# A hybrid attention layer on one core: all projected strips go through DRAM, all local heads run beside a three-pass output projection

## The chip, the cores and the metric

The kernel runs on one core of a Trainium2 chip. The metric is the time of one execution in microseconds (us) of device time, the median of several runs. The engines of a core work side by side, each in the order of its own instruction stream: TensorE (PE in the profile, with its weight loads as PEld), VectorE (DVE), ScalarE (ACT), GpSimd (POOL) and SyncE (SP). Every DMA of this kernel is issued by SP, one after the other.

## The reference

One encoder layer is applied to two sequences, a prompt of 1024 tokens and a sample of 256, each with 16 meta tokens ahead. All is float32.

```python
u = rms_norm(h, norm_w) @ w_in                    # 2048 -> 6656 = 52 strips of 128 columns
qa, ka, va, za, qb, kb, vb, zb = split(u)         # 8, 2, 2, 8, 8, 8, 8, 8 strips
qa, ka = rope(rms_norm(qa)), rope(rms_norm(ka))
ya = global_gqa(qa, ka, va) * silu(za)            # 8 heads over 2 key heads, every key
qb, kb = rms_norm(qb), rms_norm(kb)
yb = neighbourhood_attention(qb, kb, vb, rpb) * silu(zb)   # 8 heads, 8x16 window + bias + meta
return h + concat([ya, yb]) @ w_out               # 2048 -> 2048
```

## The kernel before

**Precision.** A float32 product is made as three matmuls in a rounded format: each operand is split into a high part and a low part (`split`: a cast on ACT, L65, and a subtraction on DVE, L66), and high by high, high by low and low by high are added in PSUM. Plain float32 matmuls stand only where the local heads multiply probabilities by values (L558, L618).

**First half of the projection** (`first_half`). The 16 tiles of 128 model rows are cut in two. The product of the first eight with all 52 weight strips is formed pair of strips by pair of strips with a seven-product scheme (`strassen`, matmuls L108 to L110, PSUM pool `pa`, sums by DVE at L219), and the partial sums go to DRAM (`ud`). Ahead of it `operands` loads the input (halves x1 and x2, 16 tiles each), squares on ACT (L156), adds the squares up on DVE (L158), sums over partitions on POOL (L98) and builds seven operand matrices. Beside it the generator `ahead` works off units of its own: 32 that normalise and split the second eight input tiles into DRAM (`xd`), and 64 that load, split and store the second-half weights of 32 of the 52 strips (`ws`, `wd`). These two-buffer units share DVE, ACT and SP with the products.

**Second half and attention** (`second_half`). A strip is finished by `project`: eight tiles by three token blocks (256 or 272, 512, 512), matmuls L336 to L338, then the kept sum is added (L341) and the strip is normalised (q, k), passed through silu (z) or transposed (v). Weights of the 32 strips in `AHEAD` come split from `wd`; those of the other 20 are loaded raw into the evacuation pool `ev` (7 buffers) and split there. The 8 global heads run in order, five blocks of 256 queries each (`attend`), with q, z, k and v in SBUF; after each head up to three strips of the last six local heads are projected, and these alone go to DRAM. Then the first two local heads are projected and run, and the remaining late strips follow.

**Output projection** (`outproj`). Two passes over 16 column strips: pass 0 takes the 8 global heads, pass 1 the 8 local ones, matmuls L855 to L857. The 30 blocks of the six late local heads are spread over the first 13 strips of pass 0. At strip 13 the attention pools are closed, and the local heads' results are loaded.

**What orders the work.** A scheduler that simulates the engines puts each engine's instructions in order before anything runs; the program order is its priority. At run time each engine, and SP's queue of DMAs, keeps that order: an instruction that waits holds up all that stand behind it on its engine. The kept sums `u` have four buffers (`pu`), so the load of the next one waits until an evacuation has let one go.

Of the kernel before, what the change touches and what calls it, by code (L numbers as in the profile page):

```python
# [40 lines left out]
NL = 6  # L41
FILL_A = 3
LSTR = 13
YORD = (0, 4, 1, 5, 2, 6, 3, 7)
# [9 lines left out]
AHEAD = [KA, VA, *range(ZA, ZA + 4), *range(QA, QA + 4), KA + 1, VA + 1, *range(ZA + 4, ZA + 8), *range(QA + 4, QA + 8)]  # L54
for _h in range(NH - NL, NH - NL + 3):
    AHEAD += [KB + _h, QB_ + _h, VB + _h, ZB + _h]


class Kern:
    def __init__(self, tc, io):  # L60
        self.tc, self.nc, self.io = tc, tc.nc, io

# [30 lines left out]
    def token_scale(self, half):  # L93

        nc = self.nc
        acc = self.rb[half]
        (m, r), (l, _) = self.stage("b22", 2 * half), self.stage("b22", 2 * half + 1)
        nc.gpsimd.partition_all_reduce(m, acc[:], P, RED.add)  # L98
        self.rsqrt(m, r, l)
        nc.scalar.mul(acc[:], r, -1.0)  # L100
# [41 lines left out]
    def operands(self):  # L142
# [5 lines left out]
        raw = [[self.stage(n, k) for n in ("t2", "t3")] for k in range(WCH)]  # L148
        for half in range(2):
            for kt in range(KT):  # L150
# [4 lines left out]
                acc = self.rb[half][:]  # L155
                nc.scalar.activation(sq if kt else acc, r, AF.Square, scale=DM ** -0.5)  # L156
                if kt:
                    nc.vector.tensor_tensor(out=acc, in0=acc, in1=sq, op=ALU.add)  # L158
            self.token_scale(half)
# [22 lines left out]
        for k in range(WCH):  # L182
            t2, t4 = self.stage("b22", k)
            minus(t2, norm(1, 1, k), raw[k][0][0])
            minus(t4, raw[k][0][1], t2)
            put("t2", k, t2)
            put("t4", k, t4)
        for k in range(WCH):
            b22 = raw[k][1][1]
            put("b22", k, b22)  # L190
            t3 = self.ct("t3")[:]
            minus(t3, b22, raw[k][1][0])
            put("t3", k, t3)

# [57 lines left out]
    def ahead(self):  # L252
# [17 lines left out]
        for s in AHEAD:  # L270
            for c in range(2):
                t = self.ps.tile([P, 2, WCH, P], F32R, tag="ps", name="ws")
                nc.sync.dma_start(t[:, 1].bitcast(F32), self.io["w_in"][s][:, KH + WCH * c:KH + WCH * c + WCH, :])
                self.split_tile(t)
                nc.sync.dma_start(self.wd[s][:, c], t[:].bitcast(F32))
                yield

    def first_half(self):
# [3 lines left out]
        full = [self.mixed(0, [self.wraw(self.raw, "raw") for _ in range(4)]), self.mixed(1, [t[:, j] for t in more for j in range(2)])]  # L282
        self.operands()
# [6 lines left out]
        units = 4 * KH + 2 * len(AHEAD)  # L290
        n, done = NW // 2 - 2, 0
        for i in range(n):
# [6 lines left out]
            while done * (n - 1) < units * (i + 1) and next(ahead, self) is not self:  # L299
                done += 1  # L300
# [9 lines left out]
    def weights(self, s):  # L310
        nc = self.nc
        ws = []
        with self.tc.high_priority(offset=self.woff):
            for c in range(2):
                if s in AHEAD:
                    w = self.w.tile([P, 2, WCH, P], F32R, tag="w", name="w")
                    self.lastw = nc.sync.dma_start(w[:].bitcast(F32), self.wd[s][:, c]).ins
                else:
                    w = self.wsplit(self.wload(self.wraw(self.ev, "ev"), s, 2 + c))
                ws.append(w)  # L320
        return ws
# [22 lines left out]
    def project(self, s, blocks, evac, result=None):  # L344

        ws, us = self.weights(s), self.kept(s, blocks)
# [5 lines left out]
        return result  # L352

    def project_two(self, *parts):

        ps = [[self.pp.tile([P, 512], F32, tag="pp", name="pp") for _ in range(n)] for n in (3, 1)]
        ps[1] += [self.sp.tile([P, 512], F32, tag="sp", name="pp") for _ in range(2)]
        ws = [self.weights(p[0]) for p in parts]
        for kt in range(KH):
            for p, w, part in zip(ps, ws, parts):  # L360
                for b, (o, n) in zip(p, part[1]):
                    self.tile_products(b, w, kt, o, n)
        for p, (s, blocks, evac, _) in zip(ps, parts):
            for j, ((o, n), u, b) in enumerate(zip(blocks, self.kept(s, blocks), p)):
                evac(j, self.add_kept(b, u, n), o, n)
        return [p[3] for p in parts]
# [4 lines left out]
    def qk_evac(self, u, o, n, wc, rope, hi, lo):  # L371
# [17 lines left out]
        if lo is None:  # L389
            nc.sync.dma_start(hi, r[:])  # L390
        else:
            self.split(hi, lo, r[:])
# [8 lines left out]
    def z_evac(self, u, n, dst):  # L401
# [7 lines left out]
        nc.vector.tensor_tensor(out=dst, in0=u[:], in1=a[:], op=ALU.mult)  # L409

    def meta_scores(self, pm, meta, qh, ql, scale):
# [3 lines left out]
        nc.tensor.matmul(pm, kh, qh, start=True, stop=False)  # L415
        nc.tensor.matmul(pm, kh, ql, start=False, stop=False)
        nc.tensor.matmul(pm, kl, qh, start=False, stop=True)
# [29 lines left out]
    def put_y(self, po, tot, zs, ydst):  # L447
# [8 lines left out]
        if len(zs.shape) == 3:  # L456
            nc.vector.tensor_tensor(out=y[:].rearrange("p (g r) -> p g r", g=4), in0=po[:].rearrange("p (g r) -> p g r", g=4),
                                    in1=zs, op=ALU.mult)
        else:
            nc.vector.tensor_tensor(out=y[:], in0=po[:], in1=zs, op=ALU.mult)  # L460
# [7 lines left out]
    def attend(self, q, zs, keys, meta, vals, vmeta, ydst):  # L468
# [6 lines left out]
        for p in range(nt // 2):  # L475
            ps = self.sp.tile([P, 2, QB], F32, tag="sp", name="sp")
            for i in range(2):
                kh, kl = keys[2 * p + i]
                nc.tensor.matmul(ps[:, i, :], kh, qh, start=True, stop=False)
                nc.tensor.matmul(ps[:, i, :], kh, ql, start=False, stop=False)  # L480
                nc.tensor.matmul(ps[:, i, :], kl, qh, start=False, stop=True)
# [28 lines left out]
        tot = self.all_sum(a1, sm)  # L510
        po = self.op.tile([P, QB], F32, tag="po", name="po")
        for j in range(nt):
            p, i = divmod(j, 2)
            if i == 0:
                ph = self.ph.tile([P, 2, QB], F32R, tag="ph", name="ph")
                pl = self.ph.tile([P, 2, QB], F32R, tag="pl", name="pl")
# [3 lines left out]
            nc.tensor.matmul(po[:], vl, ph[:, i, :], start=False, stop=False)  # L520
            nc.tensor.matmul(po[:], vh, pl[:, i, :], start=False, stop=False)
        nc.tensor.matmul(po[:], vmeta, pm3[:], start=False, stop=True)
        self.put_y(po, tot, zs, ydst)

    def attend_sample(self, q, zs, k, meta, vals, vmeta, tab, ydst):
# [4 lines left out]
        for w, w0 in enumerate(WIN0):  # L530
            o, c = NMETA + 32 * w0, slice(64 * w, 64 * w + 64)
            kh, kl = k[:, 0, o:o + P], k[:, 1, o:o + P]
            nc.tensor.matmul(ps[:, 0, c], kh, qh[:, c], start=True, stop=False)
            nc.tensor.matmul(ps[:, 0, c], kh, ql[:, c], start=False, stop=False)
            nc.tensor.matmul(ps[:, 0, c], kl, qh[:, c], start=False, stop=True)
# [17 lines left out]
        tot = self.all_sum(a1, sm)  # L553
        po = self.op.tile([P, QB], F32, tag="po", name="po")
        nc.tensor.matmul(po[:], vmeta, pm3[:], start=True, stop=False)
# [464 lines left out]
```

## Time and profile before

| | |
|---|---|
| three runs | 2688.16, 2689.86 (median), 2693.88 us |
| profiled execution | 2689.95 us, of which the span is 2687.8 us |
| busy | PE 2294.1, PEld 2071.1, DVE 1755.0, ACT 1057.3, POOL 509.3 us |
| DMA | 381.81 MB, 44.1% of 16 engines' span |
| mean granted TensorE clock | 0.930 |

The profiled execution is 0.09 us over the median. The busy time of PE is a union of modelled, overlapping matmuls: back to back, a matmul of 512 columns is listed with 0.39 us though the next starts 0.23 us later. A rate is therefore read from the starts. The granted clock is 1.0 or 0.5 at each moment, and a value between them in a table is a mean over a stretch.

### The profile page before, as it was taken

To read this page: it belongs to the slowest core of one execution; us is meant where nothing else is said; L and a number is where in the kernel's file an instruction comes from. 1 tells how busy PE (TensorE), PEld (TensorE's weight loads), DVE (VectorE), ACT (ScalarE), POOL (GpSimd) and SP (SyncE) were. 2 spreads that over 40 slices of the span, in tenths; PEclk is the share of its full clock that TensorE was granted. 3 is DMA by queue.
4 is the path that set the end of the run, shared out by engine and by line. 5 is a ranking of instruction groups with operands and counts; after the bars stand their busy time and mean duration, and the time that the engine had idled before them with its cause. 6 is when DMAs were issued, how large, how long until landed. Compare 5 with 4: busy or idle time off the path is not lost.

```text
span 2687.8 us, 36415 instructions
## 1 busy us (share of the span) xinstructions
PE 2294.1 (85%) x13294; PEld 2071.1 (77%) x13294; DVE 1755.0 (65%) x3096; ACT 1057.3 (39%) x2102; POOL 509.3 (19%) x250
## 2 busy tenths in 40 slices
PE   0698989899999999899678888885868999855999
PEld 0698888899998888788566777775757888755888
DVE  6866555555536989889787887885465666673221
ACT  5322333322214656556454655554333333332000
POOL 0000000000002334333233241323131122231000
PEclk9799999999999999999888899987888999956999
DMA  5166777743256333434213233222327656534432
GB/s 199 38 201 187 266 263 272 255 135 101 95 208 216 119 104 115 124 93 144 74 46 109 76 100 91 75 70 58 94 72 293 215 175 186 188 108 184 156 130 81
DMA packets 245939, 384.14 MB, mean 143 GB/s; under 512 B 64064, under 2 KB 153088, under 8 KB 242688
## 3 DMA queue, kind: packets, MB, share of 16 engines
q1 hardware_dynamic: 245760, 381.81, 44.1%
q8 instruction: 105, 1.72, 0.3%
q14 instruction: 74, 0.61, 0.1%
HBM read 236.41 MB, written 138.74 MB: 140 GB/s over the span
## 4 chain that ended last, share of the span: by engine, by line
PE 49%; DMA 19%; DVE 17%; ACT 6%; issue 4%; POOL 2%; SPq 2%; DVEq 0%; ACTq 0%; POOLq 0%
PE pp L336 5%; PE pp L855 5%; PE pp L856 5%; PE pp L857 5%; PE pp L337 5%; PE pp L338 5%; DMA ws<-in_w_in 4%; DMA wr<-in_w_in 4%; DMA wd<-ws 3%; PE pa L108 3%; PE pa L109 3%; PE pa L110 3%; DMA xs<-in_x 1%; PE po L618 1%; DVE l L78 1%
## 5 line engine op out<-in xcount | busy, mean ns | idle before, releaser
L336 PE MATMUL pp<-x,w 128*128 128x512 f32 (+2 forms) x1248 | 463.2, 372 | 79.8 <-ACT w L65 66.9
L337 PE MATMUL pp<-x,w 128*128 128x512 f32 (+2 forms) x1248 | 459.6, 369 | 0.0
L338 PE MATMUL pp<-x,w 128*128 128x512 f32 (+2 forms) x1248 | 449.3, 365 | 0.0
L65 ACT CAST w<-wr 128x512 fp32r<-128x512 f32 x286 | 172.2, 618 | 434.2 <-PE pp L857 203.3
L336 PEld LDWEIGHTS pp<-x,w 128*128 128x128 f32 x1248 | 246.7, 198 | 119.9 <-ACT w L65 71.6
L108 PE MATMUL pa<-t,w 128*128 128x320 f32 (+1 forms) x832 | 263.0, 317 | 40.2 <-DVE u L219 14.7
L375 POOL PARTITION_ALL_REDUCE ms<-l x78 | 228.1, 2925 | 316.0 <-ACT l L374 262.3
L855 PE MATMUL pp<-yh,w 128*128 128x512 f32 (+1 forms) x768 | 275.9, 359 | 14.0 <-DMA yh<-yd 14.0
L856 PE MATMUL pp<-yh,w 128*128 128x512 f32 (+1 forms) x768 | 275.3, 359 | 0.0
L857 PE MATMUL pp<-yh,w 128*128 128x512 f32 (+1 forms) x768 | 274.5, 358 | 0.0
L337 PEld LDWEIGHTS pp<-x,w 128*128 128x128 f32 x1248 | 246.4, 198 | 32.7
L66 DVE TENSOR_TENSOR w<-wr,w 128x512 fp32r<-128x512 f32 x286 | 194.9, 688 | 114.2 <-ACT w L65 113.8
L338 PEld LDWEIGHTS pp<-x,w 128*128 128x128 f32 x1248 | 241.4, 194 | 32.8
L108 PE MATMUL pa<-b,w 128*128 128x320 f32 (+1 forms) x624 | 199.1, 320 | 77.9 <-ACT b L65 60.4
L109 PE MATMUL pa<-t,w 128*128 128x320 f32 (+1 forms) x832 | 259.5, 312 | 4.3 <-DVE t L66 4.3
L110 PE MATMUL pa<-t,w 128*128 128x320 f32 (+1 forms) x832 | 259.2, 312 | 0.0
L444 POOL PARTITION_ALL_REDUCE tot<-a x80 | 169.4, 2117 | 420.2 <-DVE a L442 420.2
L109 PE MATMUL pa<-b,w 128*128 128x320 f32 (+1 forms) x624 | 196.1, 314 | 2.3 <-DVE b L66 2.3
L110 PE MATMUL pa<-b,w 128*128 128x320 f32 (+1 forms) x624 | 195.3, 313 | 0.0
L108 PEld LDWEIGHTS pa<-t,w 128*128 128x128 f32 x832 | 158.1, 190 | 46.2 <-ACT w L65 12.7
L108 PEld LDWEIGHTS pa<-b,w 128*128 128x128 f32 x624 | 119.8, 192 | 82.2 <-ACT b L65 60.8
L427 POOL PARTITION_ALL_REDUCE ma<-m x80 | 101.2, 1266 | 429.5 <-DVE m L425 418.6
(179 smaller groups left out, 5066.0 us busy)
## 6 DMA issues: line engine op xcount, KB each, us to landing
wr<-in_w_in SPq DMA_DIRECT2D x144, 256.0 KB, 3.7
wd<-ws SPq DMA_DIRECT2D x64, 512.0 KB, 3.3
w<-wd SPq DMA_DIRECT2D x64, 512.0 KB, 4.6
u<-ud SPq DMA_DIRECT2D x104, 256.0 KB, 2.9
yd<-yt SPq DMA_DIRECT2D x160, 128.0 KB, 2.1
yh<-yd SPq DMA_DIRECT2D x16, 1280.0 KB, 16.6
ud<-c SPq DMA_DIRECT2D x52, 320.0 KB, 2.6
ws<-in_w_in SPq DMA_DIRECT2D x64, 256.0 KB, 3.6
```

What stands on the lines that cost most here:

```text
L65: nc.scalar.copy(hi, full)
L66: nc.vector.tensor_tensor(out=lo, in0=full, in1=hi.bitcast(F32), op=ALU.subtract)
L108: self.nc.tensor.matmul(p, wh, xh, start=first, stop=False)
L109: self.nc.tensor.matmul(p, wh, xl, start=False, stop=False)
L110: self.nc.tensor.matmul(p, wl, xh, start=False, stop=last)
L336: self.nc.tensor.matmul(ps[:, :n], wh, xh, start=first, stop=False)
L337: self.nc.tensor.matmul(ps[:, :n], wh, xl, start=False, stop=False)
L338: self.nc.tensor.matmul(ps[:, :n], wl, xh, start=False, stop=last)
L375: nc.gpsimd.partition_all_reduce(ms[:], l[:], P, RED.add)
L855: nc.tensor.matmul(p[:, :n], wh, yh[:, o:o + n], start=i == 0, stop=False)
L856: nc.tensor.matmul(p[:, :n], wh, yl[:, o:o + n], start=False, stop=False)
L857: nc.tensor.matmul(p[:, :n], wl, yh[:, o:o + n], start=False, stop=i == 7)
```

## The change

- **Start.** x1 is loaded ahead of the first weights. Squares are added in pairs on DVE and summed over partitions by plain float32 matmuls with a matrix of ones; the reduction on POOL is gone. One operand (t4) takes a way through DRAM (`td`).
- **No weights ahead.** The 64 `ws` units leave the first half. All 52 strips load raw weights in the second half (a pool `raw` of three buffers) and split them there. The 32 input units are spread two to a pair of strips.
- **All strips to DRAM.** q and k leave split (`qd`, `kd`), v transposed (`vt`), z as it is (`zd`). An attention block loads its own 256 queries and gates (`q_load`, four buffers); keys and values are loaded once per head or group.
- **Order of the second half.** All 40 blocks of global heads are interleaved one by one with the strips; all 32 local strips are projected here, and no local block is run.
- **Probabilities by values in plain float32.** `attend` no longer splits probabilities and values: one float32 matmul per key tile in place of three.
- **Output projection in three passes** of 6, 6 and 4 heads. The 40 local blocks run beside the first two passes, 20 each, cut in two (scores, then values) at a `yield`; their matmuls and those of the passes keep the program's order (`keep_in_program_order`). Partial sums are stored and loaded once more.

The diff, cut to its core:

```diff
+OUT = ((0, 1, 2, 3, 4, 5), (6, 7, 8, 9, 10, 11), (12, 13, 14, 15))
+YTAG = (0, 1, 2, 3, 4, 5, 6, 7, 8, 0, 1, 2, 3, 4, 5, 6)
+BLOCKS = (20, 20, 0)
+    def matmul(self, *a, **kw):
+        i = self.nc.tensor.matmul(*a, **kw)
+        if self.pin:
+            self.tc.keep_in_program_order(i)
...
-                nc.scalar.activation(sq if kt else acc, r, AF.Square, scale=DM ** -0.5)
-                if kt:
-                    nc.vector.tensor_tensor(out=acc, in0=acc, in1=sq, op=ALU.add)
-            self.token_scale(half)
+                nc.scalar.activation(sq, r, AF.Square, scale=DM ** -0.5)
+                if kt % 2:
+                    nc.vector.tensor_tensor(out=sq, in0=sq, in1=before, op=ALU.add)
+                    for b in range(2):
+                        nc.tensor.matmul(sums[:, b, :HB], ones, sq[:, b], start=kt == 1, stop=kt == KT - 1)
+                before = sq
+            self.token_scale(half, sums)
+            if half == 0:
+                full = raws()
...
-        for s in AHEAD:
-            for c in range(2):
-                t = self.ps.tile([P, 2, WCH, P], F32R, tag="ps", name="ws")
...
-            while done * (n - 1) < units * (i + 1) and next(ahead, self) is not self:
+            while done < 2 * (i + 1) and next(ahead, self) is not self:
...
     def weights(self, s):
+        with self.tc.high_priority(offset=self.woff):
+            return [self.wsplit(self.wload(self.wraw(self.raw, "raw"), s, 2 + c)) for c in range(2)]
...
+        self.split(l[:].bitcast(F32R), r[:].bitcast(F32R), r[:])
+        for i, f in enumerate((l, r)):
+            nc.sync.dma_start(dst[:, i], f[:])
...
         tot = self.all_sum(a1, sm)
+        yield
         po = self.op.tile([P, QB], F32, tag="po", name="po")
         for j in range(nt):
-            p, i = divmod(j, 2)
-            if i == 0:
...
-                self.split(ph[:], pl[:], S[p][:])
-            vh, vl = vals[j]
-            nc.tensor.matmul(po[:], vh, ph[:, i, :], start=j == 0, stop=False)
-            nc.tensor.matmul(po[:], vl, ph[:, i, :], start=False, stop=False)
-            nc.tensor.matmul(po[:], vh, pl[:, i, :], start=False, stop=False)
+            self.matmul(po[:], vals[j], S[j // 2][:, j % 2, :], start=j == 0, stop=False)
...
+            for b in range(max(5, len(then))):
+                if b < 5:
+                    self.whole(self.global_block(h, b, kk, vv) if b < 4 else self.sample_block(h, sample, None))
+                if b < len(then):
+                    self.project(*self.strip(*then[b]))
+        self.project_two(*[self.strip(*x) for x in local])
...
+            step = 0.88 * units / (2 * count) if count else units + 1
+            for k in range(2 * count):
+                if k % 2 == 0:
+                    now = next(blocks)
+                    next(now)
+                else:
+                    if before is not None:
+                        for _ in before:
+                            pass
+                    before = now
+                while done < step * (k + 1):
+                    done += next(strips)
...
-                pools(es_proj, ("pu", 4), ("ev", 7))
+                pools(es_proj, ("raw", 3), ("one", 1), ("pu", 4), ("ev", 7))
```

Three places show how instructions move. The first is DVE in the middle of the first half, within one pair of strips; `w` is a weight chunk being split, `ws` a chunk split ahead for the second half, `wr` a raw chunk, and `u`, `c` and `p` are sums taken out of the PSUM banks `pa`. Before:

```order
L66 TENSOR_TENSOR ws<-ws 128x512 x2
L219 TENSOR_TENSOR u<-pa,u 128x2x320
L66 TENSOR_TENSOR w<-wr,w 128x512
L219 TENSOR_TENSOR p_3452<-u,p_3452 128x2x320
L219 TENSOR_TENSOR u<-pa,u 128x2x320
L66 TENSOR_TENSOR w<-wr,w 128x512
L66 TENSOR_TENSOR ws<-ws 128x512 x2
L66 TENSOR_TENSOR w<-wr,w 128x512
L219 TENSOR_TENSOR c_3672<-pa,u 128x2x320
```

After:

```order
L67 TENSOR_TENSOR w<-wr,w 128x512
L230 TENSOR_TENSOR u<-pa,u 128x2x320
L67 TENSOR_TENSOR w<-wr,w 128x512
L230 TENSOR_TENSOR p_3322<-u,p_3322 128x2x320
L230 TENSOR_TENSOR u<-pa,u 128x2x320
L67 TENSOR_TENSOR w<-wr,w 128x512 x2
L230 TENSOR_TENSOR c_3534<-pa,u 128x2x320
```

The `ws` rows that stood ahead of the sums, and with them their waits for a DMA, are gone.

The second place is PE in the second half, where one global block's probabilities (`ph`, `pl`, or `S` unsplit) meet the values `va`; `pp` is a strip's projection, `sp` the next scores. Before:

```order
L336 MATMUL pp<-x,w 128x512
L521 MATMUL po<-pl,va 128x256
L519 MATMUL po<-ph,va 128x256
L520 MATMUL po<-ph,va 128x256
L521 MATMUL po<-pl,va 128x256
L519 MATMUL po<-ph,va 128x256
L520 MATMUL po<-ph,va 128x256
L521 MATMUL po<-pl,va 128x256
```

After:

```order
L330 MATMUL pp<-x,w 128x512
L60 MATMUL po<-S,va 128x256 x8
L391 MATMUL tp<-ident,u 128x128 x2
L60 MATMUL sp<-q,kf 128x256 x2
L60 MATMUL po<-Pm,vm_6802 128x256
L60 MATMUL sp<-q,kf 128x256 x4
L331 MATMUL pp<-x,w 128x512
```

Eight matmuls on `S` stand where 24 on the split parts stood, and no split waits between them.

The third place is PE in the first pass of the output projection; `po<-S,vw` is a local block's values, `sp<-q,kf` another block's scores, `pp<-yh` the pass itself. Before (the scheduler's order):

```order
L856 MATMUL pp<-yh,w 128x256
L857 MATMUL pp<-yh,w 128x256
L615 MATMUL po<-Pm,vm_7131 128x256
L618 MATMUL po<-S,vw 128x128 x2
L618 MATMUL po<-S,vw 128x192 x2
L855 MATMUL pp<-yh,w 128x256
L856 MATMUL pp<-yh,w 128x256
```

After (the program's order), from one block's scores to its values:

```order
L60 MATMUL sp<-q,kf 128x128 x6
L60 MATMUL sp<-q,km 48x256 x3
L60 MATMUL sp<-q,kf 128x192 x6
L60 MATMUL pp<-yh,wo 128x512 x12
L60 MATMUL pp<-yh,wo 128x256 x6
L60 MATMUL po<-Pm,vm_6801 128x256
L60 MATMUL po<-S,vw 128x128 x2
L60 MATMUL po<-S,vw 128x192 x2
L60 MATMUL pp<-yh,wo 128x256 x12
L60 MATMUL pp<-yh,wo 128x512 x12
L60 MATMUL sp<-q,kf 128x128 x6
L60 MATMUL sp<-q,km 48x256 x3
```

A block's values now stand at a fixed distance behind its scores, with an earlier block's values and a later block's scores between them, in both of the first two passes.

More of the change, by code (lines that the diff above doesn't have):

```diff
@@ L289, in first_half @@
         ahead = self.ahead()
-        units = 4 * KH + 2 * len(AHEAD)
         n, done = NW // 2 - 2, 0
@@ L849, in out_strip @@
+                w = self.w.tile([P, 2, WCH, P], F32R, tag="w", name="wo")
+                self.split(w[:, 0, :m], w[:, 1, :m], r[:, :m])
+                for k in range(m):
+                    ws[n + k] = w[:, 0, k, :], w[:, 1, k, :]
         for blocks in (OBL[:2], OBL[2:]):
-            for i, k in enumerate(order):
-                wh, wl = ws[k]
-                yh, yl = self.ys[8 * half + k]
+            for i, h in enumerate(heads):
+                wh, wl = ws[h]
+                yh, yl = self.ys[h]
```

486 lines of the change are left out of this document (224 added, 262 removed).

## The prediction

> **What bounds the kernel now.** I read the busy times by stage first, then what PE waited for, then single rows for the prices. By stage (start and end in us; its length; busy us and instruction records of PE, PEld, DVE, ACT, POOL; granted clock; DMA share; GB/s):
>
> ```profile
> 0.00:95.00 95.00, 19.18 (x98) 17.72 (x98) 66.74 (x84) 45.15 (x65) 11.50 (x9) 0.94 0.41 141
> 95.00:265.00 170.00, 150.79 (x958) 148.50 (x958) 114.59 (x187) 50.93 (x95) 0.00 (x0) 0.94 0.54 165
> 265.00:545.00 280.00, 250.34 (x1642) 243.03 (x1643) 161.29 (x243) 87.25 (x153) 0.00 (x0) 1.00 0.78 263
> 545.00:790.00 245.00, 245.00 (x1650) 244.98 (x1649) 122.12 (x177) 53.65 (x88) 0.56 (x2) 1.00 0.35 112
> 790.00:1276.00 486.00, 457.35 (x2634) 397.65 (x2633) 406.21 (x701) 277.38 (x573) 170.06 (x73) 0.98 0.44 141
> 1276.00:1830.00 554.00, 441.11 (x2447) 384.15 (x2446) 448.57 (x773) 307.17 (x624) 171.53 (x75) 0.89 0.28 81
> 1830.00:2030.00 200.00, 148.43 (x728) 126.15 (x727) 109.98 (x198) 71.32 (x150) 51.77 (x24) 0.83 0.26 77
> 2030.00:2350.00 320.00, 303.78 (x1752) 265.51 (x1750) 206.76 (x479) 109.71 (x241) 69.14 (x46) 0.96 0.66 214
> 2350.00:2490.00 140.00, 83.64 (x380) 75.90 (x381) 74.33 (x190) 39.34 (x94) 34.72 (x23) 0.63 0.41 140
> 2490.00:2688.00 198.00, 194.47 (x1017) 167.54 (x1015) 44.42 (x72) 15.36 (x25) 0.00 (x0) 1.00 0.37 125
> ```
>
> The longest waits of PE: instruction, what it waited for, total us, times, longest:
>
> ```profile
> PE pp L336 <- ACT w L65: 66.9, 17, 10.5
> PE pa L108 <- ACT b L65: 60.4, 2, 58.0
> PE sp L479 <- ACT q L65: 49.5, 6, 18.0
> PE po L615 <- DVE Pm L437: 41.7, 9, 7.4
> PE po L555 <- DVE Pm L437: 21.0, 4, 8.3
> PE pp L855 <- DMA yh<-yd: 14.0, 2, 9.4
> ```
>
> PE is the bound in only three of these stages: from 545 to 790, most of 2030 to 2350, and from 2490 on. Elsewhere it waits, and there the clock falls as well (0.83, 0.63). The waits name the places: the operands at the start (b), weights (w), the next head's q, and a local block's probabilities (Pm). DVE, the next busiest, never passes 84% of a stage after 95 us (406.21 of 486).
>
> What PE needs when nothing holds it follows from rows of the fast clock (start, listed length, instruction):
>
> ```profile
> 2188.82 0.39 PE L857 MATMUL pp<-yh,w 128*128 128x512 f32 x1
> ...
> 2191.16 0.28 PE L855 MATMUL pp<-yh,w 128*128 128x256 f32 x1
> ...
> 2192.07 0.28 PE L615 MATMUL po<-Pm,vm 128*128 128x256 f32 x1
> 2192.19 1.26 PE L618 MATMUL po<-S,vw 128*128 128x128 f32 x8
> 2193.16 0.33 PE L533 MATMUL sp<-q,kf 128*128 128x64 f32 x1
> ```
>
> Ten matmuls of 512 columns start within 2.34 us, 0.234 each; eight of 256 within 0.91, 0.114 each, and I take 0.114 for the smaller ones and 0.121 for 272 columns. The eight records of L618 are four plain float32 matmuls with 640 columns together, in 0.97 us: 1.52 ns a column. In 545 to 790 a matmul of 320 columns takes 245/1650 = 0.1485 us.
>
> **The start.** One scale stands ahead of the first operands, a second ahead of the rest. The rows are the DMA rate, the loads, and the steps on POOL, ACT and DVE:
>
> ```profile
> GB/s 0 30 276 257 251 314 325 398 408 399 408 395 390 395 404 399 390 391 325 77 56 310 311 219 0 0 0 0 0 0 220 257 345 212 198 315 241 9 5 0
> ...
> stage<-in_x SPq DMA_DIRECT2D x32, 328.0 KB, 6.5
> wr<-in_w_in SPq DMA_DIRECT2D x10, 256.0 KB, 6.2
> ...
> 39.22 4.54 POOL L98 PARTITION_ALL_REDUCE stage<-rb  x1 [30.66 <-DVE rb L158]
> 56.30 4.97 DVE L164 SCALAR_TENSOR_TENSOR stage<-stage,nw,rb 128x656 f32<-128x656 f32 x6 [0.61 <-ACT rb L100]
> 68.25 6.06 POOL L98 PARTITION_ALL_REDUCE stage<-rb  x1 [24.50 <-DVE rb L158]
> 75.09 0.67 ACT L216 COPY u<-pa 128x640 f32<-128x640 f32 x1
> 81.45 6.59 DVE L164 SCALAR_TENSOR_TENSOR stage<-stage,nw,rb 128x656 f32<-128x656 f32 x8 [0.82 <-ACT rb L100]
> ```
>
> The first row is the DMA rate of the first 60 us in slices of 1.5 us: it reaches 400 and falls to nothing between 36 and 45, while loads wait for DVE's sums. The change halves those sums and drops the reductions, 4.54 + 6.06 us. Then x1 and the eight weight chunks ahead of its end (16 x 328 and 8 x 256 KB, 7.5 MB) need 19 us at 400 GB/s, with the start some 25; the way from the last sum to the scale, 56.30 - 39.22, less the reduction, is 12.5: the first scale comes near 38. The second, at 81.45, leads all that follows, and DVE's normalising and splitting behind it keep their length. It stands on ACT behind the two copies of the first products, the later of which ended 19.5 us behind the first scale (75.09 + 0.67), and its own steps take 7: 27 in all, so 65 in place of 81: -16. Bounds: 0, where ACT's order gives it all back, and -30, where only the loads set it (13.4 MB, 34 us). The trip of t4 through DRAM serves the last of seven products and is hidden by the six ahead of it.
>
> **The units ahead.** Their rows (busy, mean ns; idle before them and its cause):
>
> ```profile
> L66 DVE TENSOR_TENSOR ws<-ws 128x512 fp32r<-128x512 f32 x64 | 44.2, 691 | 92.4 <-ACT ws L65 92.2
> L65 ACT CAST ws<-ws 128x512 fp32r<-128x512 f32 x64 | 39.7, 620 | 195.1 <-DMA ws<-in_w_in 187.5 <-DVE wr L201 6.8 <-DVE ws L66 0.7
> ```
>
> DVE stood idle 92 us in front of `ws`, with PE's sums behind it in the queue. From 265 to 545, where they run, 1642 matmuls at 0.1485 would take 244 of the 280 us: 36 are lost, and I take -33, since the input units that remain are now spread over these strips. Bounds -10 and -40. The splits return in the second half: 64 of 0.691 on DVE, 0.620 on ACT. The first half then ends at 790 - 16 - 33 = 741.
>
> **Second half.** Records of L336, a third of the projection:
>
> ```profile
> 790.00:1276.00 486.00, 205.42 (x567) 108.33 (x567) 0.98 0.44 141
> 1276.00:1830.00 554.00, 181.57 (x490) 96.89 (x491) 0.89 0.28 81
> 1830.00:2030.00 200.00, 74.19 (x187) 40.54 (x186) 0.83 0.26 77
> ```
>
> A strip's matmul is 0.195 us on average (2496 of 512 columns, 768 of 256, 480 of 272). So the three stages needed 1701 x 0.195 + 933 x 0.114 = 438 of 486 us (90%), 1470 and 977: 398 of 554 (72%), 561 and 167: 128 of 200 (64%); together 964 of 1240 (78%).
>
> The changed second half needs 3744 projection matmuls, 730 us; 1086 smaller ones (scores, meta, transposes), 124; and 272 float32 matmuls of 256 columns at 1.52 ns, 0.388 each, 106. Sum 960: the ten local blocks leave (27 us), and float32 adds 272 x (0.388 - 0.342) = 13. The Trainium skill, "FP8 and Floating Point Precision", TensorE Precision Notes, counts four passes for true FP32, against the three here; by that rule it would be 272 x 0.114 = 31 instead of 13, an estimate, and the total 18 more. The trace does not bear it out: 640 columns took 0.97 us, where four passes at the pace of 512 columns would take 1.17.
>
> DVE loses the first row below, and ACT the second; both gain the 64 weight splits:
>
> ```profile
> L66 DVE TENSOR_TENSOR pl<-S,ph 128x512 fp32r<-128x512 f32 x136 | 93.2, 697 | 9.6 <-ACT ph L65 9.3
> L65 ACT CAST ph<-S 128x512 fp32r<-128x512 f32 x136 | 82.1, 611 | 31.5 <-PE po L520 28.5 <-DVE a L509 2.4
> ```
>
> A local block costs DVE at most 6.5 us: 2350 to 2490 has 23 reductions on POOL, two a block, so 11.5 blocks in 74.33 us. The busy sum of DVE goes from 965 us (the three stages) to 965 - 93 - 65 + 44, plus 21 for the split of the six late heads' q and k, which moves here (24 pieces of 512 columns at 0.69, 12 of half that): 872. Both sums lie well under 1240; what matters is how well they overlap. The waits for w and q stand in the later two stages, where raw weights share buffers with evacuations and a head's q is projected right ahead of its use. Now weights have buffers of their own, and q is projected a strip earlier, with z behind it. I take 88%, close under the best stage, because every strip now splits its weights, as only the worse stages did: 960/0.88 = 1091 for 1240, -149. Bounds: 93% (1032) and 72% (1333). That the stores of q and k hold their evacuation buffers for a landing longer is in the 2%.
>
> **Output projection.** Its 1536 matmuls of 512 and 768 of 256 columns need 447 us in either version. A local strip block needs 0.97 + 16 x 0.114 = 2.8, a sample block some 2.3: 40 blocks, 108. Loads of heads ahead of a pass cost 14.0 in two places, so 21 in three. The clock of 0.96 in 2030 to 2350 is 26 us at half, 13 lost, and 3 lie behind the last matmul. In that stage PE idled 16 us, some 12 of it not for loads, over 23 blocks (46 reductions): 0.5 a block, 20. Sum 612 for 658, -46: the stage of 2350 to 2490, in which no strip was left to fill, disappears. DVE then has 20 blocks (130 us) and, at 0.69 for 512 columns, some 18 us of splits and 29 of sums in a pass of 225, 79%; the third trip of the partial sums (0.66 MB each way in some 14 us a strip) is covered by PE. Bounds 585 and 700.
>
> **Sum.** 741 + 1091 + 612 = 2444, and 2.15 of the profiled execution (2689.95) outside its span: 2446. That execution lies 0.1 over the median, so nothing is corrected.
>
> **Rivals.**
> - *No better overlap.* The second half keeps its mean of 78%: 960/0.78 = 1231, total 2586. For it: the scheduler, four `u` buffers and seven `ev` buffers are the same.
> - *Fixed order stalls PE.* From 2350 to 2490, where nothing filled, PE idled 56 of 140 us over 11.5 blocks, 4.9 each. If each of 40 pinned blocks waited so, the output projection would take 612 - 20 + 196 = 788, total 2622. Against it: from scores to values stand 42 matmuls of 512 columns, 18 of 256 and two blocks' parts, some 14 us, while a block goes from its scores' bias (L591) to its last operand (L437) in 8.7 (2178.49 to 2187.19), other blocks' work on DVE included:
>
> ```profile
> 2178.49 0.41 DVE L591 SCALAR_TENSOR_TENSOR S<-sp,bt 128x256 f32<-128x256 f32 x1
> ...
> 2186.78 0.41 DVE L437 TENSOR_TENSOR Pm<-Sm,Pm 16x256 fp32r<-16x256 f32 x1
> ```
> The Trainium skill, "TensorE: Matmul & The Clock Gate", on HAM oscillation, says that idle gaps over some 3.4 us send the clock to half; the trace agrees (0.63 there), and such waits would then cost more, by an estimate half of 3.4 us a block, 68.
> - *Slower: SP's queue starves the weights.* All weights, kept sums, stores and reloads stand in one queue:
>
> ```profile
> SPq L328 <- DVE r L388: 69.2, 16, 8.5
> ...
> SPq L328 <- DVE r L388: 144.1, 15, 28.4
> ```
>
> The load of a kept sum held it for 69.2 us in 790 to 1276 and 144.1 in 1276 to 1830, up to 28.4 at once, and raw weights stood behind. Now all 52 strips load raw weights, and evacuation stores join the queue. If all run as the later two stages did, (398 + 128)/754 = 70%, the second half takes 1371: 741 + 1371 + 612 + 2 = 2726, slower by 1.3%. It decides where the second half reaches 1335, at 72%.
>
> **How the numbers follow.** Forecast 0.69, no better overlap 0.12, stalls in fixed order 0.06, starved queue 0.11, no change 0.02. A measurement of this kernel can tell about 0.2% from no change. Faster is 0.69 + 0.12 + 0.06 = 0.87, same 0.02, slower 0.11. The range: down to 2345, the good ends of start (-30), overlap (93%) and output (585) together; up to 2625, over both faster rivals; the starved queue is left out.
>
> **What would show it.** Right: first products near 45 us, the first half ending near 741 with no PE wait for L230 after 265, PE without waits for w and q in the second half at a clock over 0.95, DVE near 872 of 1091 us there, and no stretch like 2350 to 2490. Wrong: SP waiting for L382 with PE behind on w; PE waiting for Pm at the pinned matmuls; or half clock between heads.

## The result and the profile after

The changed kernel takes 2436.85 us (median of 4 runs, 2432.3 to 2439.7) beside 2690.55 for the kernel before on the same chip: a ratio of 0.9055, 95% interval 0.9037 to 0.9072. The profiled execution took 2439.7 us, its span 2437.9.

The stages of the changed kernel, in the columns of the first table of the prediction:

```profile
0.00:85.00 85.00, 45.25 (x162) 31.12 (x162) 48.41 (x64) 43.54 (x63) 0.85 (x8) 0.78 0.46 158
85.00:300.00 215.00, 188.90 (x1210) 185.46 (x1210) 143.81 (x229) 63.53 (x115) 0.00 (x0) 0.95 0.53 166
300.00:755.00 455.00, 454.76 (x3065) 454.49 (x3063) 222.96 (x321) 97.94 (x159) 0.85 (x4) 1.00 0.30 101
755.00:1276.00 521.00, 473.23 (x2532) 405.30 (x2533) 417.42 (x711) 282.91 (x588) 176.75 (x73) 0.96 0.51 159
1276.00:1815.00 539.00, 521.04 (x2842) 450.72 (x2842) 471.46 (x807) 318.12 (x661) 196.00 (x84) 0.99 0.49 147
1815.00:1880.00 65.00, 22.05 (x106) 16.99 (x105) 24.32 (x44) 18.04 (x39) 11.47 (x6) 0.68 0.71 269
1880.00:2310.00 430.00, 422.20 (x2517) 371.92 (x2517) 326.48 (x791) 150.66 (x379) 120.49 (x77) 0.99 0.83 249
2310.00:2438.00 128.00, 124.01 (x648) 104.52 (x646) 41.80 (x68) 9.34 (x15) 0.00 (x0) 1.00 0.61 209
```

PE is now the bound in most of the program: 454.76 of 455 us, 521.04 of 539, 422.20 of 430, at a clock of 0.99 or 1.0. What is left lies at the start and at two seams, around 755 and 1815. PE's longest waits say the same:

```profile
PE pp L60 <- DMA yh<-yd: 37.4, 8, 28.5
PE pa L161 <- DVE stage L159: 23.3, 8, 10.0
PE pp L329 <- ACT w L66: 20.2, 1, 20.2
PE sp L60 <- DMA q<-qd: 10.0, 7, 3.0
PE po L60 <- DVE Pm L463: 9.6, 7, 3.2
```

The 66.9 us in 17 waits for weights became one wait of 20.2, right behind the first half. The 49.5 us for q became 10.0, the 62.7 for Pm 9.6. New is one wait of 28.5 us for the heads' results at the start of the output projection.

For the accounts below the program is cut at two instructions, with the starts that the trace gives: the last matmul of the first half, and the last matmul of a projection. In the changed kernel the latter is L331, of which this is the row (records, durations in ns, first and last start):

```profile
L331 PE MATMUL pp<-x,w x1248: 275/392/632, 777.3 to 1815.1; 128*128 128x512 f32 x118, 128*128 128x256 f32 x37, 128*128 128x272 f32 x24
```

Every kernel of this study, cut so (us of the span; the third column is the output projection with the local blocks that run beside it, 30 in the kernels that start from the one before and 40 in those that start from the changed one). One of the four runs of e4 (2824.0 us) and one of e7 (4782.2 us) lay far above the others and is left out of the medians.

| kernel | first half | second half | output | median us |
|---|---|---|---|---|
| before | 793.1 | 1240.5 | 654.2 | 2690.6 |
| changed | 754.5 | 1060.6 | 622.8 | 2436.9 |
| e1 before, plain float32 values | 790.0 | 1193.1 | 640.4 | 2626.0 |
| e2 before, no weights ahead | 758.6 | 1510.5 | 653.2 | 2921.3 |
| e3 changed, weights in 7 `ev` buffers | 754.3 | 1521.1 | 621.8 | 2892.8 |
| e4 changed, blocks ahead of strips | 751.2 | 1068.5 | 620.8 | 2445.3 |
| e5 = e1 + own raw buffers | 796.3 | 1039.4 | 658.8 | 2494.2 |
| e6 = e5 + no weights ahead | 759.5 | 1075.3 | 653.5 | 2489.6 |
| e7 changed, weights in 10 `ev` buffers | 750.1 | 1460.9 | 621.6 | 2838.6 |
| e8 changed, no fixed order | 750.9 | 1057.6 | 605.4 | 2416.2 |
| e9 changed, split probabilities | 753.5 | 1100.5 | 606.6 | 2457.1 |
| e10 = e8 + raw pool low | 754.3 | 1034.2 | 592.2 | 2382.2 |
| e11 = e10 + last strips apart | 751.6 | 1036.7 | 577.0 | 2368.3 |

Stages whose code does not differ between two kernels still vary: the first half from 790.0 to 796.3 us (before, e1, e5) and from 750.1 to 754.5 (the eight kernels that start as the changed one does). The scheduler orders each program anew, which may be the reason. A single difference of 6 us or less in this table can be such variation.

### The profile page after: what moved, and what is told of

The parts are those of the page before. It is cut to its first block, busy times and chain, and to the rows that moved or that the text cites. A ratio compares the mean times of both kernels' runs of the same rounds, so it can differ in the third digit from the quotient of the medians.

```text
span 2437.9 us, 36497 instructions
## 1 busy us (share of the span) xinstructions
PE 2251.4 (92%) x13070; PEld 2020.5 (83%) x13070; DVE 1696.7 (70%) x3028; ACT 984.1 (40%) x2016; POOL 506.4 (21%) x250
## 5 line engine op out<-in xcount | busy, mean ns | idle before, releaser
L60 PE MATMUL pp<-yh,wo 128*128 128x512 f32 (+1 forms) x2304 | 470.4, 360 | 37.5 <-DMA yh<-yd 37.4
L329 PE MATMUL pp<-x,w 128*128 128x512 f32 (+2 forms) x1248 | 451.9, 362 | 25.8 <-ACT w L66 20.2
L60 PEld LDWEIGHTS pp<-yh,wo 128*128 128x128 f32 x2304 | 378.6, 189 | 106.6 <-issue 31.4
L331 PE MATMUL pp<-x,w 128*128 128x512 f32 (+2 forms) x1248 | 451.9, 363 | 0.0
L330 PE MATMUL pp<-x,w 128*128 128x512 f32 (+2 forms) x1248 | 451.7, 362 | 0.0
L369 POOL PARTITION_ALL_REDUCE ms<-l x78 | 234.8, 3010 | 370.2 <-ACT l L368 312.1
L329 PEld LDWEIGHTS pp<-x,w 128*128 128x128 f32 x1248 | 237.4, 190 | 60.8 <-ACT w L66 20.5
L67 DVE TENSOR_TENSOR w<-wr,w 128x512 fp32r<-128x512 f32 x286 | 201.3, 706 | 100.3 <-ACT w L66 99.3
L330 PEld LDWEIGHTS pp<-x,w 128*128 128x128 f32 x1248 | 237.4, 190 | 34.5
L331 PEld LDWEIGHTS pp<-x,w 128*128 128x128 f32 x1248 | 237.0, 190 | 34.4
L470 POOL PARTITION_ALL_REDUCE tot<-a x80 | 161.4, 2017 | 349.9 <-DVE a L468 338.9
L60 PE MATMUL sp<-q,kf 128*128 128x256 f32 (+2 forms) x1152 | 170.7, 285 | 16.3 <-DMA q<-qd 10.0
L60 PEld LDWEIGHTS sp<-q,kf 128*128 128x128 f32 x1152 | 155.2, 192 | 26.9 <-issue 11.9
L453 POOL PARTITION_ALL_REDUCE ma<-m x80 | 109.9, 1373 | 323.2 <-DVE m L451 290.0
```

The lines of the kernel that those rows point to most:

```text
L60: i = self.nc.tensor.matmul(*a, **kw)
L67: nc.vector.tensor_tensor(out=lo, in0=full, in1=hi.bitcast(F32), op=ALU.subtract)
L329: self.nc.tensor.matmul(ps[:, :n], wh, xh, start=first, stop=False)
L330: self.nc.tensor.matmul(ps[:, :n], wh, xl, start=False, stop=False)
L331: self.nc.tensor.matmul(ps[:, :n], wl, xh, start=False, stop=last)
L369: nc.gpsimd.partition_all_reduce(ms[:], l[:], P, RED.add)
```

## Experiments

**e1: plain float32 probabilities by values, alone.**

```diff
-            p, i = divmod(j, 2)
-            if i == 0:
...
-                self.split(ph[:], pl[:], S[p][:])
-            vh, vl = vals[j]
-            nc.tensor.matmul(po[:], vh, ph[:, i, :], start=j == 0, stop=False)
-            nc.tensor.matmul(po[:], vl, ph[:, i, :], start=False, stop=False)
-            nc.tensor.matmul(po[:], vh, pl[:, i, :], start=False, stop=False)
+            nc.tensor.matmul(po[:], vals[j], S[j // 2][:, j % 2, :], start=j == 0, stop=False)
```

> The kernel before with one part of the change alone: in the global heads probabilities times values is one plain float32 matmul per key tile instead of three, and probabilities and values are no longer split. It takes 136 casts (82 us) off ACT and 136 subtractions (93 us) off DVE and adds 13 us to PE. Theory A (buffers and order decide how well the second half overlaps, the load of DVE and ACT does not): PE's waits stay, so 2690 to 2705 us. Rival B (DVE's and ACT's load decides): the global heads' stretch shortens by most of what DVE loses there, some 60 to 90 us, so 2600 to 2630 us.

2626.0 us, 0.9778 (0.9757 to 0.9799), as rival B said: the second half lost 47 us though PE's work grew. Two rows of the kernel before, which the prediction did not use, show where a part of them was (values waiting for the split halves of the probabilities):

```profile
PE po L519 <- ACT ph L65: 12.3, 5, 6.0
PE po L521 <- DVE pl L66: 6.0, 7, 1.5
```

With e1, PE's waits for weights and q remain, but smaller (66.9 and 49.5 before). That ACT and DVE reach those operands sooner is the likely reason, which no run tests by itself:

```profile
PE pp L336 <- ACT w L65: 58.0, 16, 10.6
PE sp L479 <- ACT q L65: 36.4, 5, 11.4
```

So this edit was worth 62 us against the runs beside it, 47 of them in the half where the prediction had put a cost of 13. Another 14 are in the output projection, whose code is the same; the runs show no cause for them.

**e2: no weights split ahead, alone.**

```diff
-AHEAD = [KA, VA, *range(ZA, ZA + 4), ...]
+AHEAD = []
```

> The kernel before with another part alone: no weights are split ahead in the first half, all 52 strips load raw weights in the second half, through the 7 evacuation buffers as the late strips do. The first half should end some 30 us earlier, near 760, by every theory. Theory A (raw weights that share buffers with evacuations stall PE): the stretch that ran at 90% falls to the 72% of the strips that already worked so, 438/0.72 = 608 us for 486, in all 2690 - 30 + 122 = 2780 us (2720 to 2800). Rival B (only the load of DVE and ACT counts): 44 and 40 us return to them, about 2690 to 2705 us. Rival C (the order of blocks and strips decides): nothing is lost in the second half, 2660 us.

2921.3 us, 1.0869 (1.0851 to 1.0888): theory A had the direction, but 2720 to 2800 us was far too little; B and C are farther off. The first half ends 34 us earlier (793.1 to 758.6). The second half loses 270, and PE waits for weights in 43 places:

```profile
PE pp L334 <- ACT w L63: 191.5, 43, 14.8
```

By itself this edit would have made the kernel 8.7% slower.

**e3 and e7: raw weights back in the evacuation pool, with 7 and with 10 buffers.**

```diff
-            return [self.wsplit(self.wload(self.wraw(self.raw, "raw"), s, 2 + c)) for c in range(2)]
+            return [self.wsplit(self.wload(self.wraw(self.ev, "ev"), s, 2 + c)) for c in range(2)]
...
-                pools(es_proj, ("raw", 3), ("one", 1), ("pu", 4), ("ev", 7))
+                pools(es_proj, ("one", 1), ("pu", 4), ("ev", 7))
```

(e7 has `("ev", 10)`.)

> The changed kernel with one part undone: the pool of three raw weight buffers is left out, and raw weights go through the 7 evacuation buffers, as in the kernel before. Theory A: the second half falls from 92% (960 us of work between 775 and 1815) to 72 to 78%, 1231 to 1333 us for 1040, in all 2630 to 2730 us, with PE waiting for w and SP's queue waiting for evacuations. Rivals B and C (load of DVE and ACT, or order): no change, 2437 within 10 us.

> The changed kernel with raw weights in the evacuation pool again, as in the run at 2893 us, but with 10 buffers there in place of 7, so the same memory as 3 + 7. Theory A1 (sharing itself stalls: buffers are handed out in turn, and a weight load has to wait for the evacuation that holds the next buffer): still 2650 us or more. Rival A2 (only the number of buffers counts): 2437 to 2460 us.

2892.8 us, 1.0759 (1.0728 to 1.0790), and 2838.6 us, 1.0564 (1.0544 to 1.0583). The first lies beyond theory A's 2630 to 2730. PE's waits for weights in the second half, of e3 and then of e7:

```profile
PE pp L329 <- ACT w L66: 295.7, 44, 21.9
```
```profile
PE pp L329 <- ACT w L66: 266.5, 41, 16.8
```

Three more buffers, with the same memory as in the changed kernel, give back only 54 of 456 us. Sharing is the cause, not the count: A1 stands, A2 falls. One place in e3, on SP, ACT and PE in turn (start, length, engine, instruction, idle time before it and its cause):

```profile
1123.93 0.32 SPq L321 DMA_DIRECT2D u<-ud  x1
1124.30 0.97 SPq L122 DMA_DIRECT2D wr<-in_w_in  x2
...
1129.20 0.62 ACT L66 CAST w<-wr 128x512 fp32r<-128x512 f32 x1 [4.36 <-DMA wr<-in_w_in]
...
1129.87 0.58 PE L329 MATMUL pp<-x,w 128*128 128x256 f32 x1 [5.62 <-ACT w L66]
```

Both weight loads of a strip leave only when the evacuation of the strip before it is nearly through, PE waits 5.6 us for the landing and the cast, and the first matmul then runs at half clock (listed with 0.58 us for 256 columns in place of 0.28; the granted clock from 1129 to 1131 is 0.50). The changed kernel at about the same time:

```profile
1102.77 0.45 SPq L122 DMA_DIRECT2D wr<-in_w_in  x1
...
1104.27 0.38 SPq L122 DMA_DIRECT2D wr<-in_w_in  x1
...
1117.83 0.60 ACT L66 CAST w<-wr 128x512 fp32r<-128x512 f32 x1
...
1121.99 0.60 ACT L66 CAST w<-wr 128x512 fp32r<-128x512 f32 x1
```

The loads leave 15 and 18 us ahead of their casts, which wait for nothing. In the second half of e3 the weight loads themselves wait only 15.1 us in all in SP's queue. What holds them is mostly what stands ahead of them there: the loads of kept sums, which wait 266.2 us for L382 (147.4 in the changed kernel) and 183.4 for the gates of L402 (28.3). That the scheduler puts the weight loads so late because their buffers are shared is inferred from the edit, which changes nothing but the pools.

**e4: the order of blocks and strips undone.**

```diff
-            for b in range(max(5, len(then))):
-                if b < 5:
-                    self.whole(...)
-                if b < len(then):
-                    self.project(*self.strip(*then[b]))
+            for b in range(5):
+                self.whole(...)
+            for x in then:
+                self.project(*self.strip(*x))
```

> The changed kernel with the order undone: in the second half all five blocks of a global head are written ahead of the strips that follow it, not one strip after each block. Theory A (buffers): the scheduler still finds strips to put beside the blocks, and the stretch runs at 90% as the global heads did before: 960/0.90 = 1067 for 1040, 2437 to 2465 us. Rival C (order): back to the 78% of the second half before, 1231 for 1040, 2630 us.

2445.3 us, 0.9112 (0.9085 to 0.9138): 8 us above the changed kernel, and the second half is 8 longer. The scheduler finds the strips wherever they are written. Rival C falls.

**e5 and e6: own raw buffers, then also no weights ahead, added to e1.** The space for the pool comes from the split probabilities of e1.

```diff
-                    w = self.wsplit(self.wload(self.wraw(self.ev, "ev"), s, 2 + c))
+                    w = self.wsplit(self.wload(self.wraw(self.wr, "wr"), s, 2 + c))
...
-                pools(es_proj, ("pu", 4), ("ev", 7))
+                pools(es_proj, ("wr", 3), ("pu", 4), ("ev", 7))
```

> The kernel before with plain float32 probabilities by values (2626 us by itself) and a pool of three raw weight buffers for the 20 strips that split their weights in the second half; everything else as before. Theory A (own buffers for raw weights): its second half, 1193 us with plain float32 alone, comes near 92% busy, (960 + 27)/0.92 = 1073, in all about 2505 us (2480 to 2530). Rival (DVE's and ACT's load, or the ways q, k and z take, hold it): 2610 to 2626 us.

> The same, and no weights split ahead: all 52 strips use the three buffers. That leaves of the change the start, the way of all strips through DRAM with its order, and the output projection in three passes. Theory A: the first half loses 34 us, the second half keeps about 1073, in all near 2470 us (2445 to 2500); what is left to 2437 is then the output projection (654 against 623) and the start. Rival (sending strips through DRAM ahead of their use is what feeds PE): second half at 1193 or more, 2590 us or more.

2494.2 us, 0.9282 (0.9268 to 0.9295), and 2489.6 us, 0.9265 (0.9251 to 0.9279). Three buffers for 20 strips took 154 us off the second half of e1, with the order and the ways of q, k and z as before (132 us in all, as the first half came out 6 and the output projection 18 longer); PE there, in e5 (columns as in the stages):

```profile
796.00:1276.00 480.00, 466.72 (x2548) 401.01 (x2547) 383.77 (x655) 254.28 (x523) 164.24 (x76) 0.99 0.46 145
1276.00:1835.00 559.00, 540.92 (x2957) 465.73 (x2956) 487.03 (x853) 323.73 (x681) 212.51 (x94) 0.99 0.34 102
```

PE's waits for q fall as well, from 36.4 us in e1 to 4.8, so most of them had been a consequence of late weights. In e6 the first half gains 37 us and the second loses 36, of which one wait is half:

```profile
PE pp L334 <- ACT w L63: 18.5, 1, 18.5
```

It is the seam between the halves, now with raw weights behind the eight loads of x in SP's queue. In e5 the first weights, split ahead, are loaded in front of them.

**e8: no fixed order.** `self.pin` stays False.

> The changed kernel with the fixed order of the output projection's and local blocks' matmuls left to the scheduler. If the fixed order costs little, as forecast (0.5 us a block), the time stays at 2437 within 15 us. Rival (the fixed order is what keeps matmuls of the passes between the halves of a block): local blocks bunch again and PE waits for Pm some 2 to 5 us a block, 2480 to 2600 us. The opposite rival (the fixed order stalls PE): 2400 to 2420 us.

2416.2 us, 0.8995 (0.8980 to 0.9010): the opposite rival. Of the 21 us 17 are in the output projection, and the trace shows the place. In the 65 us behind the last projection PE is busy for 22.05 in the changed kernel (table above), and here, where the last projection matmul stands at 1808.5, for 43.66:

```profile
1808.50:1873.50 65.00, 43.66 (x199) 38.26 (x198) 45.31 (x98) 28.40 (x66) 24.75 (x13) 0.66 0.70 243
```

The scores and values of local blocks, which need no `yh`, run here while the heads' results are loaded. In the fixed order the first strip of the pass stands ahead of all of them but the first block's scores, and it waits for the results from 1827.6 to 1856.1.

**e9: probabilities split again, in the changed kernel.** The low part of the values is left out, and their high part stands in for it; so the counts and durations are those of three matmuls, but not the results.

> The changed kernel with probabilities by values in the global heads as three matmuls again, probabilities split by a cast on ACT and a subtraction on DVE (the values' low part is left out: their high part is used twice, so counts and durations are those of the kernel before). Buffers S and t are 5 and 6, as there, to make room for the split parts. In the kernel before, plain float32 alone was worth 50 us of the second half and 62 in all. If what it saves on DVE and ACT is worth that much beside own weight buffers too: second half 1060 + 40 to 50, total 2475 to 2490 us. If PE no longer waits for those engines once raw weights have buffers of their own, only PE's 13 us count: second half 1047 to 1065, total 2424 to 2445 us.

2457.1 us, 0.9148 (0.9130 to 0.9167). This total is in neither of the two ranges. The second half is 40 us longer, as the first theory said, but the output projection is 16 shorter: PE waits 17.1 us there for the heads' results in place of 37.4. The split halves are waited for in the second half:

```profile
PE po L60 <- ACT ph L66: 29.3, 16, 8.2
PE po L60 <- DVE pl L67: 13.2, 19, 2.0
```

So the gain of plain float32 in the second half does not hang on the weights. It takes a cast and a subtraction out of the chain from scores to values, and PE's queue waits 42.5 us for these two here. S and t have fewer buffers here (5 and 6 for 8 and 8), and how much of the 40 us is theirs was not separated.

**e10 and e11: the seams.** The raw pool is opened below the attention pools and serves both later stages; then also the last two strips one after the other.

```diff
-                pools(es_attn, ("k", 1), ("v", 1), ...
+                pools(es_raw, ("raw", 3))
+                pools(es_attn, ("k", 1), ("v", 1), ...
...
-        self.project_two(*[self.strip(*x) for x in local])
+        for x in local:
+            self.project(*self.strip(*x))
```

> The changed kernel without the fixed order (2416 us by itself) and with the pool of raw weights placed at the low end of SBUF, from where the first half's buffers are free earlier, one pool for both later stages. SP's queue then issues the first four raw weight loads ahead of the eight loads of x, which took 25 us at some 415 GB/s with the first weights behind them. If that queue is what PE waits for between the halves (20.2 us), the wait falls to a few us, PE then follows the x tiles at 3.2 us each, and the total is 2396 to 2404 us. If x itself is the limit: 2410 to 2416 us.

> The same, and the last two strips (q and z of the last local head) one after the other in place of side by side, so that the six evacuations behind the last projection matmul become three, those of z. Between that matmul and the first load of the output projection lay 30 us in the changed kernel. If those evacuations set it: 8 to 15 us less than the run before it. If the local blocks that now fill this gap cover it already: no difference.

2382.2 us, 0.8867 (0.8854 to 0.8880), and 2368.3 us, 0.8816 (0.8801 to 0.8832). The first is below both of its ranges, the second within its 8 to 15 us. In the changed kernel the seam stood so, on SP and ACT:

```profile
743.28 4.57 SPq L309 DMA_DIRECT2D x<-xd  x8
...
753.33 6.54 SPq L122 DMA_DIRECT2D wr<-in_w_in  x3
...
774.33 2.01 ACT L66 CAST w<-wr 128x512 fp32r<-128x512 f32 x3 [33.00 <-DMA wr<-in_w_in]
```

Eight loads of 1.3 MB at the 380 to 440 GB/s that the trace shows there are some 25 us, and the first weights came behind them. In e10:

```profile
738.33 5.81 SPq L122 DMA_DIRECT2D wr<-in_w_in  x4
744.24 3.24 SPq L309 DMA_DIRECT2D x<-xd  x4
```

PE follows without a wait, and the second half is 23 us shorter than in e8. Of the 34 us from e8 to e10 the output projection has 13 more. Its first weights are loaded from 1761 in e10 and from 1838 in e8; how much of the 13 that is was not tried. In e11 the heads' results are loaded from 1802, 14 us behind the last projection matmul at 1788, in place of 31 in the changed kernel and 30 in e10:

```profile
1802.13 2.92 SPq L794 DMA_DIRECT2D yh<-yd  x6
```

e11 is the fastest version: by the two ratios 0.8816/0.9055 = 0.974 of the changed kernel.

## Why the prediction was right, point by point

The total (2446 forecast) is 9 us off, but the stages are off by more, with both signs: first half 754.5 for 741, second half 1060.6 for 1091, output 622.8 for 612. That the sum came so close is in part luck, since these errors cancel.

**Start: the step that was mis-sized.** Forecast -16; e6 and the changed kernel give 759.5 - 754.5 = -5. Their first halves differ by the start and by how densely the 32 input units are spread, but from 300 on PE is full in both (455.00 of 455 us in e6), so the 5 us lie ahead of that. With e2 at 758.6 and the eight kernels with the new start between 750.1 and 754.5 the gain is 4 to 9 us. The two scales come at 46.0 and 76.4 instead of 38 and 65:

```profile
26.52 34.87 SPq L156 DMA_DIRECT2D stage<-in_x  x12
...
39.83 0.81 ACT L76 ACTIVATE stage<-pa,eps 128x656 f32<-128x656 f32 x1 [0.73 <-PE pa L161]
...
46.02 6.59 DVE L170 SCALAR_TENSOR_TENSOR stage<-stage,nw,rb 128x656 f32<-128x656 f32 x8
...
49.85 0.65 PE L106 MATMUL pa<-b,w 128*128 128x320 f32 x2 [2.46 <-ACT b L66]
...
76.40 6.59 DVE L170 SCALAR_TENSOR_TENSOR stage<-stage,nw,rb 128x656 f32<-128x656 f32 x8 [0.21 <-ACT rb L98]
```

The prediction let DMA and ACT's copies set these times. It had the loads of x1 and its sums end near 25 and the way from there to the scale take 12.5 us; the sums ended at 39.8, and the way took 6.2. Twelve loads of the input took 35 us to be issued: eight of the 16 tiles of each half pass through four buffers (t4), which come free only when squares on ACT, sums on DVE and plain float32 matmuls on PE have used them, and those stand among the splits and the first products. SP waited most of the 35 us for DVE's sums and PE's:

```profile
SPq L156 <- DVE stage L159: 19.3, 5, 10.6
SPq L156 <- PE pa L161: 13.2, 6, 3.6
```

A sum moved from POOL to PE joins PE's queue.

**Units ahead: right.** Forecast -33; e2 gives -34, e6 (against e5) -37. PE was full from 300 on, with no wait for L230. But the return to the second half was costed only as load on DVE and ACT and within the 88%; from e5 to e6 it costs 36 us, so that in a kernel whose weights have their own buffers the edit brings 5 us net, no more than the table's variation. The wait at the seam was missing from the sum.

**Second half: right in mechanism, with one step wrong.** Forecast 88% busy; 960/1060.6 is 91%, and 92% from the first matmul at 775 on. The forecast's main reason holds: that own buffers for raw weights do it is shown by e3 and e7 from one side (1521 and 1461 us without them) and by e5 from the other (154 us with three buffers added). That q is projected a strip earlier was named as a reason beside it; e4 and e5 give that no measurable share. DVE is busy 417.42 + 471.46 = 889 of 1060 us, near the forecast 872 of 1091.

The step that failed is the plain float32 product. The prediction charged 13 us to PE and credited DVE and ACT with smaller sums; both "lie well under 1240", and so it gave them no time of their own. The runs show a gain: 47 us of the second half before (e1), and 40 in e9. In e9 PE's waits for the split halves (29.3 + 13.2 us) are as large as that, so their place in the chain counted; in the kernel before such waits are 18.3 of the 47, and whether the rest is the chain or the load of the two engines stays open. PE's price was too low as well. Two key tiles (four records) and one matmul of 512 columns, at the fast clock:

```profile
910.43 1.02 PE L60 MATMUL po<-S,va 128*128 128x256 f32 x4
911.10 0.58 PE L331 MATMUL pp<-x,w 128*128 128x512 f32 x1
911.52 1.03 PE L60 MATMUL po<-S,va 128*128 128x256 f32 x4
```

From 910.43 to 911.52 are 1.09 us; less 0.234 for the 512 columns, 0.428 a tile, 1.67 ns a column where 1.52 was taken. Twelve such records in a row, from 1302.78 on, take 2.59 us up to the next instruction, which is 0.43 a tile. Against 0.342 for three passes that is 272 x 0.086 = 23 us where 13 were put down. The Trainium skill, "FP8 and Floating Point Precision", TensorE Precision Notes, counts four passes for true FP32; by that it would be 4 x 0.114 = 0.456, an estimate. The measurement lies between the prediction's 0.388 and this, and nearer to the page.

**Output projection: right within 11 us, in other places than it said.** From 1880 to 2310, with nearly all 40 blocks in it, PE idles 8 us where 20 were put down for blocks. The loads of heads, 21 in the sum, became most of the 43 idle us in the 65 behind the last projection (37.4 in all, 28.5 in one wait). The stretch of 140 us that nothing filled is gone, but these 65 us at a clock of 0.68 stand at the seam. From e6 to the changed kernel the three remaining parts (strips through DRAM, three passes, the start) bring 50 us of the span: 5 in the start, 15 in the second half, which gave ten local blocks away, and 31 in the output projection, which took them. How the three passes and the way through DRAM share the 31 was not tried.

**The rivals.** No better overlap: excluded at 91%. Fixed order: it does cost, but 21 us, mainly at the first strip, instead of 4.9 at each block; the forecast's reason, enough matmuls between scores and values, holds, as PE waits for no Pm from 1880 on. Starved queue: the load of a kept sum still holds SP's queue in the second half,

```profile
SPq L321 <- DVE r L382: 147.4, 30, 22.5
```

but weight loads leave ahead of their use (15 and 18 us in the place shown), and PE waits for weights only once, at the seam. Take the own buffers away, and the rival comes true and worse than its price (1521 us for 1371).

In sum, of 254 us, going from before by e1, e5 and e6: plain float32 65 by the medians of the table (62 against the runs of its own comparison), own raw buffers 132, no weights ahead 5, the rest (start, strips through DRAM and three passes) 53. The order in which edits are added matters: without own buffers for the weights, "no weights ahead" costs 231.

## What to carry to other kernels

Give prefetched operands a pool of their own. In a pool shared with evacuations the loads left late here, and three more buffers gave back only 54 of 456 us; the likely reason is that the pool hands out its buffers in turn, so that a load can't run ahead of the evacuation that holds the next one. An operation taken off a side engine can be worth much more than its share of that engine's sum says, where it stands in a chain that PE's queue waits for. After the middle is full, look at the seams: what is first in the DMA queue there, and whether an order fixed by hand keeps ready work behind a load.

## What was not expected of the hardware

A plain float32 matmul of 128 by 256 columns, with two records, took 0.428 us between others, 25% more than three rounded passes of 0.114. The prediction had read 1.52 ns a column from one group of eight records of mixed sizes in the kernel before.
